# Per-head sums in an RWKV-7 mixer: whole-array matmuls and transposes replaced by matmuls in strips of TensorE

## Chip, cores and metric

One core of a Trainium2 chip runs the whole kernel. The metric is device time in microseconds (us) of one execution, as the median of the runs shown.

## What is computed

The reference is one decoder layer on 256 tokens with 2048 features: an input projection feeds two mixers side by side (a causal pooling mixer and an RWKV-7 time mixing with 16 heads of 64 features), an output projection, a squared-ReLU MLP and a gated embedding follow. The change is in the RWKV mixer, which needs two sums over the 64 features of each head, for every token:

```python
kk = hs(k * k_k)
kk = kk / jnp.maximum(jnp.linalg.norm(kk, axis=-1, keepdims=True), 1e-12)
...
y = y + jnp.sum(r_h * k_h * r_k, axis=-1, keepdims=True) * v_h
```

The first gives one norm per head and token, by which all 64 features of the head are divided. The second gives one number per head and token, which multiplies all 64 features of v. Both are a sum over a head and then a spread back over it.

## The kernel before

**Layout.** The 16 heads are worked in two groups (gi = 0, 1) of eight heads. A tensor of a group is a tile of 128 partitions x 4 x 256: partitions are features, two heads (64 + 64) in each of the four blocks p, and the 256 columns are tokens. A sum over a head is therefore a sum over 64 partitions, which TensorE does with a matmul against ones.

**Big products.** Weights arrive in tiles of 128x1024 f32 by DMA (load_raw, L155). `split_w` splits each into a rounded high part (ScalarE, L163) and a remainder (VectorE, L164), both of type fp32r, and three products of high and low parts make one f32-like product (L176 to L178 with 256 moving columns, L185 to L187 with 512). wh, wl and raw come from rings of three tiles. `split_sb` (L168, L169) splits an activation the same way: a copy on ScalarE, then a subtraction on VectorE.

**Order of the work.** TensorE's order is written by hand (`manual_schedule` for PE). The big products are generators in a queue; `fill(us)` takes the next steps of the queue until their nominal times add up to us, and so puts big-product matmuls between two steps of the mixer; `finish(g)` takes all steps up to the end of g. A step of `gemm_cols` is three matmuls of 256 columns (nominal 0.36), one of `gemm_toks` is three of 512 columns (nominal 0.68). The order of ScalarE and VectorE is made by a planner at build time, from the order in the text and from priorities; `tc.high_priority(n)` moves work forward (weight splits have 20000, the steps of the key norms 30000, and most other work of the mixer none). `inverse` is a long VectorE computation that runs beside the big products (`beside`, `pace`). PSUM has two pools of four banks each: `mm_bank` for the big products, and `rw_bank` for the mixer, whose four banks are handed out in turn.

**Key norms** (`rwkv_k`). ScalarE squares k\*k_k into sq (L512) and loads the table of the square root (L513). After fill(5.4), eight matmuls (L524) take the squares as the stationary operand, 128 tokens at a time, and multiply with jhead, 128x2, a column of ones for each of two heads: tokens become partitions, and the result is 128x16. On it come a maximum (L527), a square root (L528) and a reciprocal (L529). After fill(3.2) two transposes (L533) turn it to 8x256, `split_sb` splits it, and after fill(1.8) eight matmuls with hsel (8x512, L543 and L544) spread each of the eight rows over the 64 partitions of its head, into two banks. VectorE multiplies each block of k with its part (L548).

**r\*k\*r_k** (`rwkv_r` makes the products in st["rk"], L585; `rwkv_values` sums them). In `rwkv_values`, sixteen records of matmuls with cen (v minus its mean over the head) go to two banks called vt (L699), which ScalarE copies to UV (L701). Then `block_sum` multiplies the 128x1024 products with jsum, a 128x128 matrix with ones in the two blocks of a head (L463): one f32 matmul of 512 columns for each half sums and spreads at once. VectorE multiplies the two results with v (L706). Only `rwkv_out` needs that, much later.

**Calls.** `rwkv_k(0)` follows the product zk0 and has zr0 as its filling; `rwkv_k(1)` has zr1. `rwkv_values(0)` stands behind the end of zr1 and of the inverse of group 0, with zp0 as filling; `rwkv_values(1)` behind `rwkv_merge(1)`, with zp1 as filling. `rwkv_core` follows some time after each.

Of the kernel before, what the change touches and what calls it, by code (L numbers as in the profile page):

```python
# [9 lines left out]
F32 = mybir.dt.float32  # L10
F32R = mybir.dt.float32r
AF = mybir.ActivationFunctionType
ALU = mybir.AluOpType
# [3 lines left out]
T = 256  # L17
# [23 lines left out]
def trunk(  # L41
# [19 lines left out]
    nc = tc.nc  # L61
# [7 lines left out]
    mc = rctx.enter_context(tc.tile_pool(name="mc", bufs=1))  # L69
# [4 lines left out]
    def rw_bank(name):  # L74
        return psr.tile([128, 512], F32, tag="rw", name=name)
# [5 lines left out]
    def col(name, j):  # L81
        o = PARAM_COLS[name] + j
        return par_sb[:, o : o + 1]
# [8 lines left out]
    ident = const.tile([128, 128], F32, name="ident")  # L92
    make_identity(nc, ident)
    ones = const.tile([128, 128], F32, name="ones")
    nc.vector.memset(ones, 1.0)
    jsum = mc.tile([128, 128], F32, name="jsum")
    cmask = mc.tile([128, 128], F32, name="cmask")
    rmask = mc.tile([128, T], F32, name="rmask")
    sbd = [mc.tile([128, 4, 128], F32, name=f"sbd{i}") for i in range(2)]
    make_block_diagonal(nc, cmask, 64)  # L100
    nc.gpsimd.tensor_copy(jsum, cmask)
    cen = mc.tile([128, 128], F32, name="cen")
    nc.vector.scalar_tensor_tensor(cen, jsum, -1.0 / 64.0, ident, op0=ALU.mult, op1=ALU.add)
    jhead = mc.tile([128, 2], F32, name="jhead")
    nc.gpsimd.tensor_copy(jhead, cmask[:, ::64])
    for r0 in (0, 64):
        make_upper_triangular(nc, cmask[r0 : r0 + 64, 0:64], val=1.0, diag=False)
        make_upper_triangular(nc, cmask[r0 : r0 + 64, 64:128], val=1.0, diag=True)
# [58 lines left out]
    def split_sb(h_ap, l_ap, src_ap):  # L167
        nc.scalar.activation(h_ap, src_ap, AF.Copy)  # L168
        nc.vector.tensor_tensor(l_ap, src_ap, h_ap.bitcast(F32), op=ALU.subtract)  # L169
# [67 lines left out]
    def advance():  # L237
        try:
            us = next(queue[0])
            pace(us)  # L240
            return us
        except StopIteration:
            queue.pop(0)
            return 0.0

    def fill(us):

        while us > 0 and queue:
            us -= advance()
# [42 lines left out]
    rp = rctx.enter_context(tc.tile_pool(name="rp", bufs=1))  # L292

    def e4(tag):
        return rp.tile([128, 4, T], F32, tag=tag, name=f"{tag}_t")

    hsel_f = rp.tile([8, 512], F32, tag="BKt", name="hsel_f")
    nc.gpsimd.memset(hsel_f, 1.0)
    nc.gpsimd.affine_select(hsel_f, hsel_f, [[1, 512]], ALU.is_ge, 0.0, base=0, channel_multiplier=-64)
    nc.gpsimd.affine_select(hsel_f, hsel_f, [[-1, 512]], ALU.is_ge, 0.0, base=63, channel_multiplier=64)  # L300
    hsel = mc.tile([8, 512], F32R, name="hsel")
    nc.gpsimd.tensor_copy(hsel, hsel_f)

    def flat(t_):
        return t_.rearrange("p a t -> p (a t)")
# [148 lines left out]
    def pair_tile(tag, name, **kw):  # L454
        t_ = rp.tile([128, 2, 512], F32R, tag=tag, name=name, **kw)
        return t_[:, 0, :], t_[:, 1, :]

    def block_sum(src, name, consume):

        s = flat(src)  # L460
        for hf in range(2):
            b = rw_bank("bsum")
            nc.tensor.matmul(b, jsum, s[:, hf * 512 : (hf + 1) * 512], start=True, stop=True)  # L463
            consume(hf, b)
# [42 lines left out]
    def rwkv_k(gi, st, zk):  # L507
        P, EI, aa = st["P"], st["EI"], st["aa"]
        sq, kkn, k2 = e4("tF"), e4("tB"), e4("tE")
        with tc.high_priority(30000):  # L510
            for p in range(4):
                nc.scalar.activation(sq[:, p, :], zk[:, p, :], AF.Square, scale=col("k_k", 4 * gi + p))  # L512
        nc.scalar.activation(warm, sq[:, 3, 0:1], AF.Sqrt)  # L513

        fill(5.4)
        nb = rw_bank("kkn")
        for hf in range(2):
            h = flat(sq)[:, hf * 512 : (hf + 1) * 512]
            for j in range(2):
                for tt in range(2):  # L520
                    o = tt * 8 + (2 * hf + j) * 2
                    ts_ = slice(j * T + tt * 128, j * T + (tt + 1) * 128)
                    first = hf == 0 and j == 0 and tt == 0
                    nc.tensor.matmul(nb[:, o : o + 2], h[:, ts_], jhead, start=first, stop=True, skip_group_check=True)  # L524
        rn = rp.tile([128, 16], F32, tag="rn", name=f"rn{gi}")
        with tc.high_priority(30000):
            nc.vector.tensor_scalar_max(rn, nb[:, 0:16], 1e-24)  # L527
            nc.scalar.activation(rn, rn, AF.Sqrt)  # L528
            nc.vector.reciprocal(rn, rn)  # L529
        fill(3.2)  # L530
        nb = rw_bank("rnT")
        for tt in range(2):
            nc.tensor.transpose(nb[0:8, tt * 128 : (tt + 1) * 128], rn[:, tt * 8 : tt * 8 + 8], ident)  # L533
        rnh, rnl = (t_[0:8, 0:T] for t_ in pair_tile("tE", f"rnp{gi}"))
        with tc.high_priority(30000):
            split_sb(rnh, rnl, nb[0:8, 0:T])
        fill(1.8)
        for half in range(2):
            b = rw_bank("rnb")
            for j in range(2):  # L540
                p = half * 2 + j
                o = b[:, j * T : (j + 1) * T]
                nc.tensor.matmul(o, hsel[:, p * 128 : (p + 1) * 128], rnh, start=j == 0, stop=False, skip_group_check=True)  # L543
                nc.tensor.matmul(o, hsel[:, p * 128 : (p + 1) * 128], rnl, start=False, stop=True, skip_group_check=True)  # L544
            for j in range(2):
                p = half * 2 + j
                with tc.high_priority(30000):
                    nc.vector.scalar_tensor_tensor(  # L548
                        kkn[:, p, :], zk[:, p, :], col("k_k", 4 * gi + p), b[:, j * T : (j + 1) * T], op0=ALU.mult, op1=ALU.mult
                )  # L550
# [140 lines left out]

    def rwkv_values(gi, st, zv):

        uvs = [rp.tile([128, 2, 8, 64], F32, tag=f"q{i}", name=f"UV{gi}_{i}") for i in range(2)]
        UV = [uvs[c // 2][:, c % 2] for c in range(4)]
        for tt in range(2):
            b = rw_bank("vt")
            for p in range(4):
                nc.tensor.matmul(b[:, p * 128 : (p + 1) * 128], zv[:, p, tt * 128 : (tt + 1) * 128], cen, start=True, stop=True)  # L699
            for i in range(2):  # L700
                nc.scalar.activation(flat3(UV[2 * tt + i])[64:128], b[i * 64 : (i + 1) * 64, :], AF.Copy)  # L701
        bon = st["rk"]
        bf, vf = flat(bon), flat(zv)
        block_sum(
            st["rk"], f"rk{gi}",
            lambda hf, b: nc.vector.tensor_tensor(  # L706
                bf[:, hf * 512 : (hf + 1) * 512], b, vf[:, hf * 512 : (hf + 1) * 512], op=ALU.mult
            ),
        )
        st["UV"] = UV  # L710

    def rwkv_core(gi, st):
# [88 lines left out]
    def flat3(t_):  # L801
        return t_.rearrange("s h i -> s (h i)")
# [588 lines left out]
```

## Time and profile before

| | |
|---|---|
| median of three runs (lowest, highest) | 1204.59 us (1203.06, 1206.01) |
| profiled execution: its time | 1204.86 us |
| its span, first to last instruction | 1203.1 us |
| mean granted clock of TensorE | 0.997 |
| instructions | 18401 |

The profile comes from one execution. Engines are PE (TensorE matmuls), PEld (its weight loads), DVE (VectorE), ACT (ScalarE), POOL (GpSimd) and SP (the DMA queue's engine). A row of instructions gives start and duration in us, engine, line, operation, output <- inputs, shapes, a count, and in brackets the idle time before it and what ended it. A row of a group gives the shapes and count, then busy us and mean ns of one, then idle time before and its causes. A row of the chain gives start, duration and what ran. Matmuls are pipelined, so the time that one takes in a row of them is the distance between two starts and not its duration. A stretch of the chain has this distance in it.

### The profile page before, as it was taken

Reading aid. Unit: us, or ns where it says so; the run is one execution under the profiler, and the core shown is the slowest. Engines: PE = TensorE matmul, PEld = TensorE weight load, DVE = VectorE, ACT = ScalarE, POOL = GpSimd, SP = SyncE. Lnnn points to the kernel's source line nnn. Section 1 sums busy time; section 2 is a strip of 40 time slices with the busy share of each in tenths; the row PEclk is TensorE's granted clock in tenths of the full one; section 3 lists DMA queues with packets and bytes.
Section 4 is the critical chain, followed back from the end, with each engine's and each line's share of the span. In section 5 each row is a group of like instructions: output and inputs, shape, how many; then the busy total and the mean of one; then the engine's idle time right before and its main releaser. Section 6 shows DMA issues by size and latency. Waiting matters only on the chain.

```text
span 1203.1 us, 18401 instructions
## 1 busy us (share of the span) xinstructions
PE 1183.2 (98%) x7070; PEld 1015.0 (84%) x7070; DVE 872.9 (73%) x1186; ACT 674.7 (56%) x1203; POOL 15.5 (1%) x65
## 2 busy tenths in 40 slices
PE   7999999999999999999999999999999999999997
PEld 5999988987888888888888888888888887887886
DVE  6887987964566666666878887666667788788753
ACT  5957556565545545555545554555555555468743
POOL 3100000000000000000000000000000000000000
PEclk9999999999999999999999999999999999999999
DMA  7363543354365565565656666665565666666841
GB/s 275 124 195 113 175 141 107 107 187 142 120 211 175 175 192 184 185 191 180 192 200 205 206 194 217 185 191 181 187 192 168 194 205 204 229 203 200 271 139 70
DMA packets 60616, 216.88 MB, mean 180 GB/s; under 512 B 6768, under 2 KB 7536, under 8 KB 60144
## 3 DMA queue, kind: packets, MB, share of 16 engines
q1 hardware_dynamic: 60240, 215.20, 55.5%
q8 instruction: 55, 0.90, 0.3%
q10 hardware_dynamic: 288, 0.51, 0.1%
q14 instruction: 33, 0.27, 0.1%
HBM read 213.59 MB, written 2.10 MB: 179 GB/s over the span
## 4 chain that ended last, share of the span: by engine, by line
PE 89%; DVE 6%; DMA 2%; ACT 2%; issue 1%; ACTq 0%; DVEq 0%
PE u_w L1016 20%; PE d_p L1085 15%; PE u_w L1020 10%; PE d_w L1085 4%; PE d_d L1085 4%; DMA raw_d<-in_w_ffn_down_dram 2%; PE gt_b L187 2%; PE gt_b L186 2%; PE gt_b L185 2%; PE wag_b L346 1%; PE zp_b L185 1%; PE zv_b L176 1%; PE zp_b L187 1%; PE zp_b L186 1%; PE o_b L186 1%; PE o_b L185 1%
## 5 line engine op out<-in xcount | busy, mean ns | idle before, releaser
L1016 PE MATMUL u_w<-h,wh_u 128*128 128x512 f32 x1024 | 362.1, 399 | 0.0
L1020 PE MATMUL u_w<-h,wl_u 128*128 128x256 f32 x1024 | 287.7, 281 | 0.0
L164 DVE TENSOR_TENSOR wl_u<-raw_u,wh_u 128x1024 fp32r<-128x1024 f32 x128 | 156.7, 1224 | 122.2 <-ACT wh_u L163 122.2
L163 ACT ACTIVATE wh_u<-raw_u 128x512 fp32r<-128x512 f32 x256 | 147.6, 624 | 173.4 <-issue 137.0
L1016 PEld LDWEIGHTS u_w<-h,wh_u 128*128 128x128 f32 x1024 | 192.4, 188 | 47.9
L1020 PEld LDWEIGHTS u_w<-h,wl_u 128*128 128x128 f32 x1024 | 193.4, 189 | 0.0
L1085 PE MATMUL d_p<-wh_d,yd 128*128 128x512 f32 x480 | 154.5, 389 | 0.8 <-ACT wh_d L163 0.8
L163 ACT ACTIVATE wh_d<-raw_d 128x512 fp32r<-128x512 f32 x160 | 89.1, 620 | 36.8 <-issue 18.5
L1085 PEld LDWEIGHTS d_p<-wh_d,yd 128*128 128x128 f32 x480 | 90.1, 188 | 20.0 <-ACT wh_d L163 1.2
L164 DVE TENSOR_TENSOR wl_d<-raw_d,wh_d 128x1024 fp32r<-128x1024 f32 x80 | 95.4, 1220 | 14.3 <-ACT wh_d L163 13.9
L1085 PE MATMUL d_p<-wl_d,yd 128*128 128x512 f32 x240 | 93.6, 390 | 0.0
L1085 PE MATMUL d_d<-wh_d,yd 128*128 128x512 f32 x160 | 55.8, 389 | 0.0
L1085 PEld LDWEIGHTS d_p<-wl_d,yd 128*128 128x128 f32 x240 | 45.1, 188 | 9.7 <-DVE wl_d L164 0.6
L1138 ACT ACTIVATE th_d<-t_d 128x1024 fp32r<-128x1024 f32 x24 | 25.4, 1058 | 47.6 <-DVE t_d L1135 30.2
L1085 PE MATMUL d_w<-th_d,ys 128*128 128x512 f32 x144 | 48.2, 389 | 0.0
L1142 ACT ACTIVATE th_d<-t_d 128x1024 fp32r<-128x1024 f32 x24 | 25.4, 1059 | 35.4 <-DVE t_d L1140 31.2
L1143 DVE TENSOR_TENSOR tl_d<-t_d,th_d 128x1024 fp32r<-128x1024 f32 x24 | 29.4, 1225 | 19.9 <-ACT th_d L1142 19.6
L1132 ACT ACTIVATE w7h_d<-raw_d 128x1024 fp32r<-128x1024 f32 x24 | 25.4, 1059 | 23.4 <-DMA raw_d<-in_w_ffn_down_dram 13.8
L187 PE MATMUL gt_b<-wh_gt,h 128*128 128x512 f32 x96 | 37.8, 393 | 0.0
L176 PE MATMUL zv_b<-hTh,wh_zv 128*128 128x256 f32 x128 | 37.7, 294 | 0.0
L176 PE MATMUL zr_b<-hTh,wh_zr 128*128 128x256 f32 x128 | 37.5, 293 | 0.0
L185 PE MATMUL gt_b<-wh_gt,h 128*128 128x512 f32 x96 | 37.5, 390 | 0.0
(582 smaller groups left out, 2622.8 us busy)
## 6 DMA issues: line engine op xcount, KB each, us to landing
raw_u<-in_w_ffn_up_dram SPq DMA_DIRECT2D x128, 512.0 KB, 3.5
raw_d<-in_w_ffn_down_dram SPq DMA_DIRECT2D x128, 512.0 KB, 3.9
raw_gt<-in_w_ple_gate_dram SPq DMA_DIRECT2D x24, 512.0 KB, 4.2
raw_zk<-in_w_in_dram SPq DMA_DIRECT2D x16, 512.0 KB, 3.4
raw_zr<-in_w_in_dram SPq DMA_DIRECT2D x16, 512.0 KB, 3.5
raw_zv<-in_w_in_dram SPq DMA_DIRECT2D x16, 512.0 KB, 3.4
raw_zp<-in_w_in_dram SPq DMA_DIRECT2D x16, 512.0 KB, 3.4
raw_o<-in_w_out_dram SPq DMA_DIRECT2D x16, 512.0 KB, 4.1
```

The costliest lines, as they stand in the source:

```text
L163: nc.scalar.activation(wh[:, a * 512 : (a + 1) * 512], raw[:, a * 512 : (a + 1) * 512], AF.Copy)
L164: nc.vector.tensor_tensor(wl, raw, wh.bitcast(F32), op=ALU.subtract)
L176: nc.tensor.matmul(o, w_h, ah, start=first and ct % 2 == 0, stop=False, skip_group_check=True)
L185: nc.tensor.matmul(o, a_h, wh[:, 0:n], start=first, stop=False)
L186: nc.tensor.matmul(o, a_h, wl[:, 0:n], start=False, stop=False)
L187: nc.tensor.matmul(o, a_l, wh[:, 0:n], start=False, stop=last)
L1016: nc.tensor.matmul(bank[:, ct, :].rearrange("p (s t) -> p s t", s=2), wh[:, c], hl, start=k == 0, stop=False, skip_group_check=True,)
L1020: nc.tensor.matmul(bank[:, ct, 0:T], wl[:, c], hl[:, 0, :], start=False, stop=k == 15, skip_group_check=True)
L1085: nc.tensor.matmul(o, l, r, start=first, stop=last, skip_group_check=True)
L1132: nc.scalar.activation(ha, ra, AF.Copy)
L1138: nc.scalar.activation(th[0], t[0], AF.Copy)
L1143: nc.vector.tensor_tensor(tl[1], t[1], th[1].bitcast(F32), op=ALU.subtract)
```

## The change

- `block_sum`, jsum and the two transposes go. `jhead` becomes 128x32, with zeros beyond its first two columns; `hsel` becomes 128x128, in each 32 rows of which the first two hold ones for the two heads of a block.
- `head_sums` makes four f32 matmuls of 256 columns, one for each block p, with jhead stationary; block p's result goes to partitions 32p to 32p+31 of one bank (a column strip). The result is 128x256, of which two rows in each 32 are used.
- `head_spread` takes the two halves h and l of such a tile. For each half and each p it multiplies rows 32p to 32p+31 (a row strip) with the same rows of hsel, into four banks, first all four of h, then all four of l.
- `rwkv_k`: maximum, root, reciprocal and split now work on 128x256 directly; the fills 3.2 and 1.8 become one of 4.6 between the split and the spread.
- `rwkv_values`: the r\*k\*r_k sums stand first, then `split_sb` without priority, fill(2.0), the spread, and four products with v of 128x256 in place of two of 128x512; vt follows.

```diff
-    jsum = mc.tile([128, 128], F32, name="jsum")
...
-    nc.gpsimd.tensor_copy(jsum, cmask)
...
-    nc.vector.scalar_tensor_tensor(cen, jsum, -1.0 / 64.0, ident, op0=ALU.mult, op1=ALU.add)
-    jhead = mc.tile([128, 2], F32, name="jhead")
-    nc.gpsimd.tensor_copy(jhead, cmask[:, ::64])
+    nc.vector.scalar_tensor_tensor(cen, cmask, -1.0 / 64.0, ident, op0=ALU.mult, op1=ALU.add)
+    jhead = mc.tile([128, 32], F32, name="jhead")
+    nc.gpsimd.memset(jhead, 0.0)
+    nc.gpsimd.tensor_copy(jhead[:, 0:2], cmask[:, ::64])
...
-    def block_sum(src, name, consume):
...
+    def head_sums(src, name):
+
+        b = rw_bank(name)
+        for p in range(4):
+            nc.tensor.matmul(b[p * 32 : (p + 1) * 32, 0:T], jhead, src[:, p, :], start=True, stop=True)
+        return b[:, 0:T]
+
+    def head_spread(h, l, name):
+
+        banks = [rw_bank(f"{name}{p}") for p in range(4)]
+        for part in (h, l):
+            for p in range(4):
+                r = slice(p * 32, (p + 1) * 32)
+                nc.tensor.matmul(banks[p][:, 0:T], hsel[r], part[r], start=part is h, stop=part is l)
+        return [b[:, 0:T] for b in banks]
...
+        nb = head_sums(sq, "kkn")
+        rn = rp.tile([128, T], F32, tag="rn", name=f"rn{gi}")
+        rnh, rnl = (t_[:, 0:T] for t_ in pair_tile("tE", f"rnp{gi}"))
         with tc.high_priority(30000):
-            nc.vector.tensor_scalar_max(rn, nb[:, 0:16], 1e-24)
+            nc.vector.tensor_scalar_max(rn, nb, 1e-24)
             nc.scalar.activation(rn, rn, AF.Sqrt)
             nc.vector.reciprocal(rn, rn)
...
+            split_sb(rnh, rnl, rn)
+        fill(4.6)
+        rnb = head_spread(rnh, rnl, "rnb")
+        for p in range(4):
+            with tc.high_priority(30000):
+                nc.vector.scalar_tensor_tensor(
+                    kkn[:, p, :], zk[:, p, :], col("k_k", 4 * gi + p), rnb[p], op0=ALU.mult, op1=ALU.mult
...
     def rwkv_values(gi, st, zv):
 
+        bon = st["rk"]
+        nb = head_sums(bon, "bsum")
+        bp = rp.tile([128, 2, T], F32R, tag="sq", name=f"bs{gi}")
+        bh, bl = bp[:, 0], bp[:, 1]
+        split_sb(bh, bl, nb)
+        fill(2.0)
+        for p, b in enumerate(head_spread(bh, bl, "bon")):
+            nc.vector.tensor_tensor(bon[:, p, :], b, zv[:, p, :], op=ALU.mult)
...
-        bon = st["rk"]
-        bf, vf = flat(bon), flat(zv)
-        block_sum(
```

More of the change, by code (lines that the diff above doesn't have):

```diff
@@ L295, in e4 @@
         return rp.tile([128, 4, T], F32, tag=tag, name=f"{tag}_t")
-    hsel_f = rp.tile([8, 512], F32, tag="BKt", name="hsel_f")
+    hsel_f = rp.tile([128, 128], F32, tag="BKt", name="hsel_f")
     nc.gpsimd.memset(hsel_f, 1.0)
-    nc.gpsimd.affine_select(hsel_f, hsel_f, [[1, 512]], ALU.is_ge, 0.0, base=0, channel_multiplier=-64)
-    nc.gpsimd.affine_select(hsel_f, hsel_f, [[-1, 512]], ALU.is_ge, 0.0, base=63, channel_multiplier=64)
-    hsel = mc.tile([8, 512], F32R, name="hsel")
+    for p in range(4):
+        hs_ = hsel_f[p * 32 : (p + 1) * 32]
+        nc.gpsimd.affine_select(hs_, hs_, [[1, 128]], ALU.is_ge, 0.0, base=0, channel_multiplier=-64)
+        nc.gpsimd.affine_select(hs_, hs_, [[-1, 128]], ALU.is_ge, 0.0, base=63, channel_multiplier=64)
+    hsel = mc.tile([128, 128], F32R, name="hsel")
     nc.gpsimd.tensor_copy(hsel, hsel_f)
@@ L456, in pair_tile @@
         return t_[:, 0, :], t_[:, 1, :]
-    def block_sum(src, name, consume):
[L460 to L464, printed above, removed]
+    def head_sums(src, name):
[10 more added lines that the diff above has]
+        return [b[:, 0:T] for b in banks]
     def prod3(o, lh, ll, rh, rl, first=True, last=True):
@@ L515, in rwkv_k @@
         fill(5.4)
[L516 to L524, printed above, removed]
@@ L525, in rwkv_k @@
-        rn = rp.tile([128, 16], F32, tag="rn", name=f"rn{gi}")
+        nb = head_sums(sq, "kkn")
+        rn = rp.tile([128, T], F32, tag="rn", name=f"rn{gi}")
+        rnh, rnl = (t_[:, 0:T] for t_ in pair_tile("tE", f"rnp{gi}"))
         with tc.high_priority(30000):
-            nc.vector.tensor_scalar_max(rn, nb[:, 0:16], 1e-24)
+            nc.vector.tensor_scalar_max(rn, nb, 1e-24)
             nc.scalar.activation(rn, rn, AF.Sqrt)
             nc.vector.reciprocal(rn, rn)
-        fill(3.2)
@@ L531, in rwkv_k @@
[L531 to L549, printed above, removed]
+            split_sb(rnh, rnl, rn)
@@ L550, in rwkv_k @@
+        fill(4.6)
+        rnb = head_spread(rnh, rnl, "rnb")
+        for p in range(4):
+            with tc.high_priority(30000):
+                nc.vector.scalar_tensor_tensor(
+                    kkn[:, p, :], zk[:, p, :], col("k_k", 4 * gi + p), rnb[p], op0=ALU.mult, op1=ALU.mult
                 )
@@ L701, in rwkv_values @@
                 nc.scalar.activation(flat3(UV[2 * tt + i])[64:128], b[i * 64 : (i + 1) * 64, :], AF.Copy)
-        bon = st["rk"]
-        bf, vf = flat(bon), flat(zv)
-        block_sum(
[L705 to L709, printed above, removed]
         st["UV"] = UV
```

## The prediction

> **What bounds the kernel.** I began with the page: busy times, then the shares of the chain that ended last.
>
> ```profile
> PE 1183.2 (98%) x7070; PEld 1015.0 (84%) x7070; DVE 872.9 (73%) x1186; ACT 674.7 (56%) x1203; POOL 15.5 (1%) x65
> PE 89%; DVE 6%; DMA 2%; ACT 2%; issue 1%; ACTq 0%; DVEq 0%
> ```
>
> TensorE (PE) is busy for 98% of the span and is 89% of the chain. So PE time that goes is time won, and any new wait of PE is time lost, wherever it stands. Next, the busy times by stage where the change works (columns: stretch, length, busy PE, PEld, DVE, ACT, POOL, granted clock, DMA share, GB/s).
>
> ```profile
> 140.00:150.00 10.00, 9.20 (x75) 8.62 (x74) 9.69 (x23) 6.80 (x14) 0.00 (x0) 1.00 0.47 171
> 150.00:156.00 6.00, 6.00 (x38) 5.87 (x38) 6.00 (x9) 3.72 (x8) 0.24 (x1) 0.72 0.37 117
> 164.00:176.00 12.00, 12.00 (x70) 9.43 (x70) 10.28 (x17) 7.97 (x15) 0.00 (x0) 1.00 0.40 132
> 262.00:283.00 21.00, 21.00 (x272) 16.99 (x271) 6.07 (x10) 11.85 (x22) 0.00 (x0) 1.00 0.26 88
> ```
>
> The key norms of head group 1 fall at 140 to 150 us, where DVE has 0.31 us of 10 free; the r\*k\*r_k sums of group 0 at 164 to 176, where DVE and ACT are also well filled; those of group 1 at 262 to 283, where DVE has 15 us free. The second row has a granted clock of 0.72. The timeline of PE shows what came before it.
>
> ```profile
> 148.56 0.38 PE L543 MATMUL rnb<-rnp,hsel 8*128 8x256 f32 x1
> 149.61 0.38 PE L544 MATMUL rnb<-rnp,hsel 8*128 8x256 f32 x1 [0.67 <-DVE rnp L169]
> ...
> 151.93 0.28 PE L177 MATMUL zr_b<-hTl,wh_zr 128*128 128x256 f32 x1
> 152.05 0.33 PE L178 MATMUL zr_b<-hTh,wl_zr 128*128 128x256 f32 x1
> 152.17 0.41 PE L176 MATMUL zr_b<-hTh,wh_zr 128*128 128x256 f32 x1
> ...
> 155.37 0.37 PE L176 MATMUL zr_b<-hTh,wh_zr 128*128 128x256 f32 x1
> 155.58 0.28 PE L177 MATMUL zr_b<-hTl,wh_zr 128*128 128x256 f32 x1
> ```
>
> Matmuls of 256 columns follow each other every 0.12 us (151.93, 152.05). At 148.56 PE waits 1.05 us for DVE's half of the split norms, 0.93 more than its pace. From 152.17 to 155.37 the pace is 0.21: 3.2 us for work of about 1.8, a loss of 1.4. So a wait of about 1 us cost 0.93 + 1.4 us. The rule beside it, from the Trainium skill, "TensorE: Matmul & The Clock Gate", Part 1 (The HAM clock gate): the clock halves after an idle window of about 3.4 us. Here 1.05 us of waiting was followed by the low clock, so the trace is harsher than the page.
>
> **The change on PE.** What goes, per head group:
>
> ```profile
> 59.18 1.68 PE kkn L524 x16
> 64.20 0.22 PE rnT L533 x2
> 66.49 0.38 PE L543 MATMUL rnb<-rnp,hsel 8*128 8x256 f32 x1
> 67.62 0.39 PE L176 MATMUL zr_b<-hTh,wh_zr 128*128 128x256 f32 x1
> 164.25 1.78 PE vt L699 x16
> 166.03 1.72 PE bsum L463 x4
> ```
>
> Norm sums 1.68, transposes about 0.2 (two of the four records stand in the row; the phase's neighbours leave no more), spread 67.62 - 66.49 = 1.13, r\*k\*r_k sums 1.72: 4.73 us. Each f32 matmul is two records (8 matmuls, x16).
>
> What comes: four f32 matmuls of 256 columns in four column strips (head_sums), and eight split ones of 256 columns in four row strips (head_spread), each twice per group. The trace has strips already.
>
> ```profile
> 239.62 1.73 PE gt L835 x8
> 241.35 1.06 PE gt L839 x8
> 202.65 0.62 PE sm L767 x16
> 203.27 0.93 PE rym L780 x16
> ```
>
> L835 and L839 are four f32 matmuls of 256 columns each; L835 uses the whole array, L839 alternates between two 32-row strips: 1.06 against 1.73. L767 alternates between two column halves, L780 stays in one: 0.62 against 0.93 for the same 16 records. So strips do overlap. 1.06 is five of L835's eight 0.216 us passes: the two records of one matmul go one after the other, and the second overlaps the next strip's first. The same order is in head_sums, so I take 1.06, and 0.2 for the seams around a strip phase (an estimate: the spread's 1.13 is 0.17 more than eight steps of 0.12): 1.26. For the spread I take 0.61 (1.06 / 1.73) of 1.13, or 0.7, seams included as in the 1.13. New: 2 x 1.26 + 2 x 0.7 = 3.9 us. Saved 0.8 per group, **-1.6 us** in all.
>
> Bounds: with all four strips at once, sums 1.73 / 4 + 0.2 = 0.63 and spread 1.13 / 4 + 0.2 = 0.48, so 2.2 per group and -5.0 in all. With no overlap, 1.93 and 1.33, so 6.5 per group and +3.6. I take the middle, nearest to L839. For the upper bound speaks the Trainium skill, "TensorEngine Tiling (Array Packing)", Key Properties: changing the tiling mode drains TensorE. The change has eight strip phases.
>
> **The change on DVE and ACT.** The norms now stand as 128x256 instead of 128x16.
>
> ```profile
> L529 DVE RECIPROCAL rn<-rn 128x16 f32<-128x16 f32 x2 | 0.5, 252 | 0.7 <-ACT rn L528 0.7
> L811 DVE RECIPROCAL gv<-gv 128x8 f32<-128x8 f32 x4 | 0.7, 185 | 1.7 <-ACT gv L810 1.7
> L548 DVE SCALAR_TENSOR_TENSOR tB_t<-zk_t,par_sb,rnb 128x256 f32<-128x256 f32 x8 | 3.3, 464 | 0.7 <-PE rnb L544 0.7
> L169 DVE TENSOR_TENSOR hTl<-tA_t,hTh 128x256 fp32r<-128x256 f32 x4 | 1.6, 424 | 0.4 <-ACT hTh L168 0.2
> L168 ACT ACTIVATE hTh<-tA_t 128x256 fp32r<-128x256 f32 x4 | 1.6, 417 | 0.6 <-DVE tA_t L404 0.5
> ```
>
> Eight more columns cost the reciprocal 67 ns, 8.4 ns each; 240 more give 252 + 2016 = 2.27 us. If the cost levels off it is that of another 128x256 operation, 0.42. I take 2.0, near the slope. The chain from sums to spread is then maximum 0.46, square root 0.42, reciprocal 2.0, copy 0.42, subtraction 0.42: 3.7 us on free engines, and fill(4.6) is 13 steps of three matmuls, 4.7 us of cover. On free engines nothing waits. But the engines have queues.
>
> ```profile
> 141.74 2.36 DVE L164 TENSOR_TENSOR wl_zr<-raw_zr,wh_zr 128x1024 fp32r<-128x1024 f32 x2
> 142.77 1.28 ACT L513 ACT_TABLE_LOAD   x1
> 144.02 0.17 DVE L527 TENSOR_SCALAR rn<-kkn 128x16 f32<-128x16 f32 x1
> 144.93 0.25 DVE L529 RECIPROCAL rn<-rn 128x16 f32<-128x16 f32 x1
> 147.31 2.00 DVE L661 STREAM_TRANSPOSE T1G<-X 32x512 f32<-32x512 f32 x2
> 149.17 0.39 DVE L169 TENSOR_TENSOR rnp<-rnT,rnp 8x256 fp32r<-8x256 f32 x1
> ```
>
> Key norms, group 1: PE ends the sums near 141.9, and the maximum stays behind two weight splits and the root behind the table load, so the reciprocal begins near 145 and ends near 147. Copy and subtraction follow, the latter behind one split of 1.2 us: ready at 148.4 to 149. PE arrives at 141.9 + 5 = 146.9. The four high-half spreads cover 0.3. New wait about 1.5 against 0.93 now: **+0.6**, from -2.3 (no wait, no low clock) to +2. Behind the subtraction stand the weight splits of the next products; behind the wait of ACT's k2 scaling (L552) stands the next rounding of weights. The ring of three weight tiles hides that; without it PE would be late by as much as they are, which the +2 holds. Key norms, group 0: sums end near 60.4, PE arrives at 65.1, and the 3.7 on free engines end at 64.1; one weight split ahead on DVE (1.2, half the row) and one rounding ahead on ACT (0.6, half of L701's row below) make it 65.9: **+0.8** (0 to 2.3, more if the clock falls).
>
> **r\*k\*r_k.** Before, nothing on PE waited for its sums. Now PE computes sums, waits for ACT's rounding and DVE's subtraction, spreads, and only then does vt; fill(2.0) gives three steps of 0.7 us. Neither half of the split has raised priority. What stands in ACT's and DVE's queues there:
>
> ```profile
> 165.93 1.04 ACT L669 ACTIVATE SC<-tmp 32x1024 f32<-32x1024 f32 x1
> 167.35 1.06 ACT L669 ACTIVATE SC<-tmp 32x1024 f32<-32x1024 f32 x1
> 168.42 1.19 ACT L701 ACTIVATE UV<-vt 64x512 f32<-64x512 f32 x2
> 168.32 1.21 DVE L577 TENSOR_TENSOR AR<-zr_t,tA_t 128x1024 f32<-128x1024 f32 x1
> 169.46 1.26 DVE L585 SCALAR_TENSOR_TENSOR tF_t<-zr_t,par_sb,tE_t 128x256 f32<-128x256 f32 x3
> 170.65 1.27 DVE L706 TENSOR_TENSOR ybuf<-bsum,zv_t 128x512 f32<-128x512 f32 x2
> ```
>
> The first half of vt (L701's input) is done near 165.1, yet ACT came to it at 168.42; L706's is done at 167.75, and DVE came at 170.65. The split takes the same places: rounding at 168.4, subtraction between 169.3 and 171. PE starts the sums at 164.25, ends them at 165.5 and the fill at 167.6. Wait 1.7 to 3.7; I take 3.0, and with it a low clock of 1.4 to 1.5: **+4.5** (0 to +5.3). All of PE's products stand behind it. Group 1 (262 to 283) has idle DVE and ACT: 0. In both groups vt takes the bank of the first spread, so it waits for one product of 0.43 (L548's size, less what the last spreads cover): 0.3 each, **+0.6**. The bank sums' own DVE work grows from two 128x512 to four 128x256 products, beside PE. The POOL edits at the start, and the weights of `cen`, are needed tens of us later: 0; uncovered they would cost a few tenths.
>
> Sum: -1.6 + 0.6 + 0.8 + 4.5 + 0.6 = +4.9. The profiled execution took 1204.86 us, 1.76 of them outside its span of 1203.1: 1209.8. It lies 0.27 above the median 1204.59, so the forecast for a median is **1209.5**.
>
> **Rivals.**
> Queues let the split through. If ACT and DVE take the r\*k\*r_k split about as it comes, the 4.5 falls to about 1: 1206. For it: DVE has 1.7 us free in 164 to 176. Against: L701 and L706.
>
> Strips pay and all covers hold, ending faster: -1.6 or up to -5.0, the present wait and low clock gone (-2.3), +0.6: 1201 to 1198. For it: 3.7 against 4.7 on free engines. Against: the subtraction now comes 7 us after the sums (142.2 to 149.17). The Trainium skill, "TensorE: Matmul & The Clock Gate", Measured speedup vs the span model, has four row strips 3.07 times as fast; by it the sums would take 1.73 / 3.07 = 0.56 us, an estimate, and this rival would be nearer its lower end. No run here shows four strips.
>
> The strips don't overlap, so the change doesn't do what it says: PE +3.6 in place of -1.6, so 1214.7. Against: L839, L767. The Trainium skill's same page, Part 3, What overlaps and what doesn't, lets weights load beside a matmul only in another row group, which would hold for the column strips; L767's 0.62 against 0.93 speaks otherwise.
>
> Low clock three times: the norms of group 0 also wait over 1 us: 1209.5 + 1.4 = 1211.
>
> **How the numbers follow.** Forecast 0.45 (own range 1207 to 1212.5), queues let it through 0.26, pays 0.12, no overlap 0.09, low clock three times 0.08. Range 1202 to 1214: it leaves out most of "no overlap" and the lower end of "pays". A measurement tells about 0.3%, 3.6 us, from no change: slower means above 1208.2, faster below 1201. Slower: 0.38 of the forecast and 0.09 + 0.08, 0.55. Faster: most of "pays", 0.09. Same: 0.36.
>
> **What would show it.** L524's successor near 1.06 us on the chain; a reciprocal of 128x256 near 2 us; PE waiting for DVE's subtraction of the r\*k\*r_k sums near 168 us, and a granted clock below 1 behind it; none near 270. It is wrong if the planner puts that split ahead of L669 and L585, or the reciprocal takes 0.4.

## The result, and the profile after

The changed kernel takes 1212.74 us (median of 5 runs, 1211.58 to 1214.21), the kernel before 1204.59 (1200.28 to 1206.2 in 5): a ratio of 1.0073 [1.0051, 1.0096], so 8.15 us lost. The profiled execution took 1212.74 us, 1211.0 of them span. The busy times of the page:

```profile
PE 1182.3 (98%) x7074; PEld 1012.2 (84%) x7074; DVE 876.4 (72%) x1192; ACT 676.3 (56%) x1205; POOL 18.0 (1%) x71
```

PE's busy time is 0.9 us less than before, in a span that is 7.9 longer. The loss is not work: it is waiting, and a lower clock behind the wait. The view of PE's waits in the changed kernel (what waited for what: us in total, times, longest):

```profile
...
PE bon L472 <- DVE bs L168: 5.3, 1, 5.3
...
PE vt L696 <- DVE tF_t L690: 1.1, 1, 1.1
PE rnb L472 <- ACT rnp L167: 1.0, 1, 1.0
...
PE rnb L472 <- DVE rnp L168: 0.7, 1, 0.7
```

The line of bon is the prediction's wait: the spread of the r\*k\*r_k sums (bon) stands until DVE has subtracted the high half (bs). The same stretches as before the change:

```profile
140.00:150.00 10.00, 7.57 (x57) 6.42 (x55) 9.76 (x19) 6.83 (x13) 0.00 (x0) 0.95 0.56 174
150.00:156.00 6.00, 6.00 (x43) 6.00 (x43) 5.68 (x8) 3.41 (x7) 1.10 (x2) 0.81 0.44 144
164.00:176.00 12.00, 6.36 (x32) 5.22 (x31) 9.04 (x17) 3.74 (x7) 0.00 (x0) 0.73 0.27 87
262.00:283.00 21.00, 19.92 (x224) 16.72 (x223) 9.37 (x14) 9.94 (x19) 0.00 (x0) 1.00 0.43 142
```

In the third stretch PE was busy for 12 us of 12 before, now 6.36, and the granted clock fell from 1.00 to 0.73. To put the loss in its place, compare where the same work starts on PE (us from the span's start):

| start of | before | after | shift | gained or lost since the row above |
|---|---|---|---|---|
| norm sums, group 0 | 59.02 | 59.03 | 0 | |
| norm sums, group 1 | 140.71 | 139.49 | -1.2 | -1.2: norms of group 0 |
| r\*k\*r_k and vt, group 0 | 164.09 | 163.11 | -1.0 | +0.2: norms of group 1 |
| scores, group 1 | 175.21 | 183.90 | +8.7 | +9.7: r\*k\*r_k of group 0 |
| merge (qm), group 1 | 266.76 | 275.93 | +9.2 | +0.5 |
| h2t of the next stage | 357.64 | 365.44 | +7.8 | -1.4: r\*k\*r_k of group 1 and GEMM steps left |
| end | 1203.1 | 1211.0 | +7.9 | +0.1 |

Of the +9.7, 2.1 us are three GEMM steps that the new fill(2.0) brings forward; they come back in the row of -1.4, which is +0.7 of its own less these 2.1. So one place lost about 7.6 us. The timeline of PE there, and of DVE and ACT in the same microseconds:

```profile
163.11 0.64 PE L463 MATMUL bsum<-ybuf,jhead 128*32 128x256 f32 x8
...
165.96 0.39 PE L472 MATMUL bon<-bs,hsel 32*128 32x256 f32 x3
171.68 0.79 PE L472 MATMUL bon<-bs,hsel 32*128 32x256 f32 x5 [5.33 <-DVE bs L168]
172.78 3.68 PE L696 MATMUL vt<-cen,zv_t 128*128 128x128 f32 x16 [0.31 <-DVE ybuf L690]
```

```profile
165.09 1.19 DVE L163 TENSOR_TENSOR wl_zp<-raw_zp,wh_zp 128x1024 fp32r<-128x1024 f32 x1
166.21 0.46 DVE L311 SCALAR_TENSOR_TENSOR zr_t<-zr_b,par_sb,zr_t 128x255 f32<-128x255 f32 x1
166.60 0.46 DVE L574 SCALAR_TENSOR_TENSOR tF_t<-zr_t,par_sb,tE_t 128x256 f32<-128x256 f32 x1
166.99 1.21 DVE L566 TENSOR_TENSOR AR<-zr_t,tA_t 128x1024 f32<-128x1024 f32 x1
168.12 1.26 DVE L574 SCALAR_TENSOR_TENSOR tF_t<-zr_t,par_sb,tE_t 128x256 f32<-128x256 f32 x3
169.31 2.04 DVE L654 STREAM_TRANSPOSE tmp<-X 64x512 f32<-64x512 f32 x2
171.26 0.37 DVE L168 TENSOR_TENSOR bs<-bsum,bs 128x256 fp32r<-128x256 f32 x1
```

```profile
165.23 0.39 ACT L167 ACTIVATE bs<-bsum 128x256 fp32r<-128x256 f32 x1
171.39 2.12 ACT L658 ACTIVATE SC<-tmp 32x1024 f32<-32x1024 f32 x2 [5.76 <-DVE tmp L654]
```

Read the three together. ACT has the high half ready near 165.6, and PE uses it at 165.96 for three of the four blocks (x3). The fourth, by the order in which banks are handed out, goes to the bank of the sums, which DVE's subtraction still has to read, and then come the four of the low half, which the subtraction makes (x5). That subtraction takes DVE 0.37 us, but stands last in DVE's order, behind 5.6 us of work that PE has no use for yet. PE moves again at 171.68, and vt then takes 3.44 us (172.78 to 176.22, where the next GEMM record starts) for 1.78 before. The low clock behind the wait (stretches of the changed kernel, the clock is the third number from the right):

```profile
170.00:175.00 5.00, 3.01 (x15) 2.72 (x16) 3.04 (x7) 2.11 (x2) 0.00 (x0) 0.50 0.00 0
175.00:180.00 5.00, 5.00 (x25) 4.35 (x24) 1.04 (x1) 2.36 (x5) 0.00 (x0) 0.88 0.02 3
```

PE is busy for 3.01 us of the first stretch and for all of the second, so the low clock costs about 3.01 x 0.5 + 5 x 0.12 = 2.1 us.

The strips themselves do what they say, and more than I counted. The sums of group 0's norms and what follows them on PE, the spread in group 1, and the reciprocal in the view of the tile rn (ns: shortest/median/longest):

```profile
59.03 0.64 PE L463 MATMUL kkn<-tF_t,jhead 128*32 128x256 f32 x8
59.60 0.38 PE L175 MATMUL zr_b<-hTh,wh_zr 128*128 128x256 f32 x1
...
280.90 0.51 PE L472 MATMUL bon<-bs,hsel 32*128 32x256 f32 x8
```

```profile
L531 DVE RECIPROCAL rn<-rn x2: 1746/1750/1753, 62.1 to 145.2; 128x256 f32<-128x256 f32 x2
```

A phase of sums takes 0.57 us (59.03 to 59.60), a phase of spread 0.51 (the length of its row; PE waits behind it). That holds where PE finds its inputs ready. At the norms it does not always: the spread of group 0 lasts from 64.74 to 65.59, 0.85 us, and the sums of group 1 last 1.00, because the squares of their last block come late from ACT. PE then waits for a weight split that it now reaches sooner:

```profile
64.74 0.93 PE L472 MATMUL rnb<-rnp,hsel 32*128 32x256 f32 x8
65.59 0.39 PE L175 MATMUL zr_b<-hTh,wh_zr 128*128 128x256 f32 x1
...
139.49 1.06 PE L463 MATMUL kkn<-tF_t,jhead 128*32 128x256 f32 x8
140.49 0.39 PE L175 MATMUL zr_b<-hTh,wh_zr 128*128 128x256 f32 x1
...
141.72 0.39 PE L177 MATMUL zr_b<-hTh,wl_zr 128*128 128x256 f32 x1 [0.73 <-DVE wl_zr L163]
```

### The profile page after: what moved, and what is told of

Its sections match the earlier page's. It is cut to its first block, busy times and chain, and to the rows that moved or that the text cites. A ratio compares the mean times of both kernels' runs of the same rounds, so it can differ in the third digit from the quotient of the medians.

```text
span 1211.0 us, 18418 instructions
## 1 busy us (share of the span) xinstructions
PE 1182.3 (98%) x7074; PEld 1012.2 (84%) x7074; DVE 876.4 (72%) x1192; ACT 676.3 (56%) x1205; POOL 18.0 (1%) x71
## 4 chain that ended last, share of the span: by engine, by line
PE 70%; DVE 3%; DMA 2%; ACT 1%; issue 0%; DVEq 0%; ACTq 0%
PE u_w L1005 20%; PE d_p L1074 14%; PE u_w L1009 10%; PE d_w L1074 4%; PE d_d L1074 4%; DMA raw_d<-in_w_ffn_down_dram 2%; PE gt_b L185 2%; PE gt_b L184 2%; PE gt_b L186 2%; PE o_b L185 1%; PE o_b L184 1%; PE o_b L186 1%; DVE wl_d L163 0%; PE o0a_b L184 0%; DVE w7l_d L1122 0%
## 5 line engine op out<-in xcount | busy, mean ns | idle before, releaser
L177 PE MATMUL zr_b<-hTh,wl_zr 128*128 128x256 f32 x128 | 37.1, 290 | 0.7 <-DVE wl_zr L163 0.7
```

Of the source, the lines that this page charges most:

```text
L177: nc.tensor.matmul(o, w_l, ah, start=False, stop=last, skip_group_check=True)
```

## The experiments

The theory I took to the chip: the loss is the **order of DVE's queue** at the r\*k\*r_k sums of group 0, where the split has no priority, plus the low clock behind the wait; the strips gain. A further guess hung on it: that the two long reciprocals of the norms (1.75 us each) push the inverse's last transposes (L654) in front of that subtraction and make the wait longer. Rivals: DVE is simply full there, and order only decides who waits; the strip phases or the longer chain of the norms cost the time.

### e1_prio_split_prod: priority for the split and the products

```diff
-        split_sb(bh, bl, nb)
+        with tc.high_priority(30000):
+            split_sb(bh, bl, nb)
...
-            nc.vector.tensor_tensor(bon[:, p, :], b, zv[:, p, :], op=ALU.mult)
+            with tc.high_priority(30000):
+                nc.vector.tensor_tensor(bon[:, p, :], b, zv[:, p, :], op=ALU.mult)
```

> The split of the r*k*r_k sums and the four products behind it get raised priority, in both groups; nothing else changes. Theory (order of DVE's queue): PE's wait of 5.3 us for the subtraction in group 0 falls below 1 us, the low clock behind it goes too; 1212.7 - 5.3 - 2.5 to 3 = about 1204 to 1205. Rival (DVE is full, the order only decides who waits): the inverse's last transposes land later by what the split and the products take (about 0.4 + 4 x 0.4 us), PE waits for them elsewhere before the scores, and the time stays within 2 us of 1212.7. Rival (the strip phases themselves cost): the wait goes, but the time stays above 1208.

Measured: 1204.43 us, ratio to the kernel before 1.0 [0.999, 1.0011]. The whole loss of 8.3 us against 1212.74 is gone. PE's timeline in this kernel:

```profile
161.02 0.64 PE L463 MATMUL bsum<-ybuf,jhead 128*32 128x256 f32 x8
...
163.86 0.51 PE L472 MATMUL bon<-bs,hsel 32*128 32x256 f32 x8
...
165.65 2.05 PE L698 MATMUL vt<-cen,zv_t 128*128 128x128 f32 x16 [1.28 <-DVE ybuf L692]
```

and DVE's, where the subtraction and the products now stand ahead of the transposes:

```profile
163.34 0.40 DVE L168 TENSOR_TENSOR bs<-bsum,bs 128x256 fp32r<-128x256 f32 x1
...
165.19 1.40 DVE L692 TENSOR_TENSOR ybuf<-bon,zv_t 128x256 f32<-128x256 f32 x4
...
170.82 2.29 DVE L654 STREAM_TRANSPOSE tmp<-X 64x512 f32<-64x512 f32 x2
```

No wait in front of the spread, none of the low clock (1.00 in every stretch from 140 to 185). PE did not wait for the later transposes elsewhere. The theory holds, and the rival "the wait only moves" falls for the large wait. What is left is 1.28 us at vt here and 1.1 in group 1.

### e11_prio_split: the same for the split alone

```diff
-        split_sb(bh, bl, nb)
+        with tc.high_priority(30000):
+            split_sb(bh, bl, nb)
```

> The changed kernel with raised priority for the split alone, not for the products behind it. Theory (DVE's order decides for each link of the chain): PE's wait of 5.3 us in front of the spread goes, but vt now waits for the bank of the first spread, whose product stands behind the same last transposes of the inverse on DVE until about 171 us, so PE waits 4 us or more at vt with the low clock behind it, and the time stays at 1210 to 1212.7. Rival (the split alone was what stood late): 1204 to 1205, level with e1_prio_split_prod.

Measured: 1212.66 us, ratio 1.0072 [1.0058, 1.0086]. PE in this kernel:

```profile
166.94 0.51 PE L472 MATMUL bon<-bs,hsel 32*128 32x256 f32 x8
...
173.00 3.78 PE L697 MATMUL vt<-cen,zv_t 128*128 128x128 f32 x16 [5.55 <-DVE ybuf L691]
```

The spread is on time, and vt waits 5.55 us for its bank in place of 5.33 for the split: the product that frees the bank stands behind the same transposes. Each link of the chain must have its place in DVE's order; mending one moves the wait to the next, at the same price.

### e2_norms_only, e3_values_only: one half of the change at a time

Norms alone; `rwkv_values`, block_sum and jsum are those of before the change:

```diff
-        bon = st["rk"]
-        nb = head_sums(bon, "bsum")
...
+        block_sum(
+            st["rk"], f"rk{gi}",
```

> Only the key norms take the strips; the r*k*r_k sums are as before the change. Theory: the norms gained 1.2 us in group 0 and lost 0.2 in group 1, so 1203 to 1204.5, and the first scores of group 1 start within 2 us of the kernel before. Rival (the longer chain of the norms delays the inverse, and that is the loss): 1207 or more, with a new PE wait behind the inverse's last transposes.

Measured: 1201.42 us, ratio 0.9976 [0.9965, 0.9987]: **faster than both kernels**, by 2.9 us against the one before. What the longer chain of the norms costs in waits (1.0 and 0.7 us in group 1) is less than what the strips win there.

r\*k\*r_k alone; the key norms, with 128x2 and 8x512 constants of their own, are those of before the change:

```diff
-        nb = head_sums(sq, "kkn")
...
+                    nc.tensor.matmul(nb[:, o : o + 2], h[:, ts_], jhead2, start=first, stop=True, skip_group_check=True)
...
-        rnb = head_spread(rnh, rnl, "rnb")
...
+                nc.tensor.matmul(o, hsel8[:, p * 128 : (p + 1) * 128], rnh, start=j == 0, stop=False, skip_group_check=True)
```

> Only the r*k*r_k sums take the strips; the key norms are as before the change. Theory: the wait for the subtraction in group 0 stays, at about 3 us since the inverse's last transposes stand earlier in DVE's queue, with a low clock behind it: 1208 to 1210. If the norms have no part in that wait: 5.3 us again and about 1213. If the wait needs the norms (they alone push the transposes in front of it): below 1 us and about 1203.

Measured: 1211.24 us, ratio 1.0057 [1.0044, 1.007]. PE in this kernel:

```profile
168.34 0.39 PE L481 MATMUL bon<-bs,hsel 32*128 32x256 f32 x3 [2.59 <-ACT bs L169]
170.65 0.79 PE L481 MATMUL bon<-bs,hsel 32*128 32x256 f32 x5 [1.92 <-DVE bs L170]
```

The wait is 4.5 us, not 3. It needs nothing of the norms. Here the transposes were early (DVE ended the last at 165.3), and other work stood in front of the subtraction just the same: it starts at 170.19. The two halves do not add: -2.9 and +7.0 make +4.1, and the change costs 8.15. The norms bring PE to the r\*k\*r_k sums earlier, but there the end of the wait is set by DVE, which lets PE go at 170.65 here and at 171.68 in the changed kernel. What PE gains ahead of such a wait is lost in it.

### e4_no_division

```diff
-            nc.vector.reciprocal(rn, rn)
+            nc.vector.tensor_scalar_mul(rn, rn, 4e-7)
```

> The changed kernel with the reciprocal of the norms (2 x 1.75 us on DVE) replaced by a multiplication by a constant (about 0.25 to 0.4 us each): the division is left out, so the keys are scaled by a constant times their norm. Theory: DVE wins about 1.4 us per group, the inverse's last transposes move ahead of where they stood, PE's wait in group 0 falls from 5.3 to about 3, the waits at the norms of group 1 (1.0 + 0.7) go: about 1207 to 1209. If the reciprocal has no part in it: only the waits at the norms go, 1211. If the reciprocal is all of it: 1203.

Measured: 1210.29 us, ratio 1.0048 [1.0035, 1.006]. PE in this kernel:

```profile
166.06 0.58 PE L472 MATMUL bon<-bs,hsel 32*128 32x256 f32 x3 [4.36 <-ACT bs L167]
168.44 0.79 PE L472 MATMUL bon<-bs,hsel 32*128 32x256 f32 x5 [1.79 <-DVE bs L168]
```

My further guess falls. The transposes did move forward, and the waits at the norms went, but the wait at the spread became 6.2 us: now ACT's rounding came late as well, behind the copies of the inverse's result (L658), which have their input sooner. PE arrives 4 us earlier than in the changed kernel and is let go 3.2 us earlier (168.44 for 171.68). Wherever the inverse's transposes stand in the three kernels whose split has no priority (the changed one, r\*k\*r_k alone, no division), DVE comes to the subtraction only after the r products.

### e8_no_strips

The same sums and spreads on the whole array, on top of the priorities of the first experiment (jfull has the two columns of jhead at 96, hfull is hsel with all rows of the other strips zero):

```diff
-        for p in range(4):
-            nc.tensor.matmul(b[p * 32 : (p + 1) * 32, 0:T], jhead, src[:, p, :], start=True, stop=True)
+        for p in (3, 0, 1, 2):
+            nc.tensor.matmul(b[0 : (p + 1) * 32, 0:T], jfull[:, 96 - p * 32 :], src[:, p, :], start=p == 3, stop=p == 2, skip_group_check=True)
...
-                nc.tensor.matmul(banks[p][:, 0:T], hsel[r], part[r], start=part is h, stop=part is l)
+                nc.tensor.matmul(banks[p][:, 0:T], hfull[:, p, :], part, start=part is h, stop=part is l)
```

> The kernel of e1_prio_split_prod with the same matmuls on the whole array: the sums have 128 rows of weights and up to 128 columns that are zero but for one head pair and accumulate in one bank, the spread has 128 rows of weights that are zero but for one strip; the results are the same. Theory (four strips work at the same time: a phase of sums takes 0.57 us against 1.7, a phase of spread 0.6 to 0.85 against 1.1): four phases of each cost 4 x 1.15 + 4 x 0.4 = about 6 more, so 1210, less what they shorten the waits for the split and for the bank, 1208 to 1210. Rival (the strips save nothing, the gain of the norms is the missing transposes): 1204 to 1205.

Measured: 1211.76 us, ratio 1.0066 [1.0049, 1.0082]; 7.3 us more than with strips. Sums and spread in this kernel:

```profile
59.08 2.32 PE L468 MATMUL kkn<-tF_t,jfull 128*128 128x256 f32 x8
61.06 0.47 PE L175 MATMUL zr_b<-hTh,wh_zr 128*128 128x256 f32 x1
...
171.12 1.11 PE L476 MATMUL bon<-bs,hfull 128*128 128x256 f32 x8
```

1.98 us for 0.57, and about 1.1 for 0.51: four phases of each make 4 x (1.41 + 0.6) = 8.0, which the 7.3 nearly are (the waits shift too: 2.3 + 0.6 us for 1.0 + 1.0 at the norms, 0.4 + 0.5 for 1.3 + 1.1 at vt; and the clock of 150 to 156 us is 0.72 for 1.00). So the strips are worth their price: they gain in the order of 7 us over the same matmuls without them. (The old r\*k\*r_k sums needed no spread, and so are not what this compares with.)

### e5, e6, e7: more GEMM steps in the gaps

Three kernels try to close what is left of the waits by moving queued GEMM steps into them. In the first, fill(1.4) stands between the spread and vt of the kernel with priorities; in the second, fill(4.6) of the norms becomes fill(6.3) in the kernel with the norms alone; the third has both edits on the kernel with priorities.

```diff
+        fill(1.4)
         uvs = [rp.tile([128, 2, 8, 64], F32, tag=f"q{i}", name=f"UV{gi}_{i}") for i in range(2)]
...
-        fill(4.6)
+        fill(6.3)
```

> The kernel of e1_prio_split_prod with 1.4 us of queued GEMM steps put between the spread of the r*k*r_k sums and the products with cen (vt), in both groups. Theory (what is left of the loss is vt's wait for the bank that the first spread holds until its product is done, 1.28 us in group 0 and 1.08 in group 1): both waits go and 1204.4 falls by about 2.4 to 1202. Rival (the steps that fill the gap are missing later as cover, in the group's core): a new wait of about the same size there, and 1204.

> The kernel of e2_norms_only (key norms in strips, r*k*r_k as before the change) with fill(6.3) in place of fill(4.6) between the sums and the spread of the norms, in both groups. Theory: the waits of 1.0 and 0.7 us for the split of the norms in group 1 and 0.3 in group 0 go: 1201.4 falls by about 1.5 to 2 to 1199.5. Rival (the inverse's first steps and the scores start later and are late instead, or the steps are missing later): 1201 or more.

> Both of the last two edits on the changed kernel with raised priority: fill(6.3) in the norms and 1.4 us of GEMM steps ahead of vt. Theory: the two gains add, 1204.4 - 2.4 - 1.7 = about 1200.3, level with the norms alone in strips. If the strips also gain in r*k*r_k: below 1199. If cover is short: 1202 or more.

Measured: 1204.99 us (ratio 1.0009 [0.9998, 1.002]), 1201.62 (0.998 [0.9967, 0.9994]) and 1203.42 (1.0002 [0.9989, 1.0014]). None gains on its base (1204.43, 1201.42 and 1204.43) what the waits had promised. The profile of the second shows one way in which that happens. The norms alone, two stretches:

```profile
150.00:160.00 10.00, 10.00 (x85) 10.00 (x84) 10.00 (x11) 5.00 (x10) 1.10 (x2) 1.00 0.47 156
160.00:170.00 10.00, 10.00 (x54) 8.08 (x53) 10.00 (x16) 4.20 (x9) 0.00 (x0) 1.00 0.41 135
```

DVE is busy for all of these 20 us. With the larger fill PE no longer waits at the norms; then, in the view of PE's waits and in the stretch behind it:

```profile
PE sc L602 <- DVE ybuf L705: 1.3, 1, 1.3
```

```profile
175.00:180.00 5.00, 5.00 (x28) 3.77 (x28) 1.70 (x3) 3.22 (x10) 0.00 (x0) 0.71 0.38 113
```

The scores of group 1 wait 1.3 us for a bank that DVE's product holds, with a clock of 0.71 behind it. The gap was closed and opened again 25 us later. In this execution the rival is right for these last 1 to 2 us: from 150 to 170 us **DVE is the second bound**, and work that PE does in one gap opens another. In the third kernel the wait came back at the spread itself:

```profile
164.23 0.50 PE L472 MATMUL bon<-bs,hsel 32*128 32x256 f32 x5 [1.06 <-DVE bs L168]
```

That PE's gaps can't be closed at all is not shown. The profiles of the first and the third kernel come from executions of 1209.55 and 1209.91 us, 4.6 and 6.5 above their medians, and that excess stands in a stage that no edit touches: from the first d_w to the first pp_b (the second product of the MLP, long after the mixer) they take 508.3 and 510.6 us, the kernel with priorities 503.8. Where the edits act, from the norm sums of group 0 to h2t, the third takes 296.4 us for 298.2 in its base, so there the moved steps closed part of the gaps; its median shows 1.0 us. The first takes 298.9 for 298.2: its waits at vt are down from 2.4 to 0.5 us, but its clock was 0.91 and 0.87 from 140 to 156 us.

### e9, e10: r\*k\*r_k in strips where DVE is free

The norms in strips, and r\*k\*r_k in strips in group 1 alone (products with priority), without and with fill(1.4) ahead of vt:

```diff
+        if gi == 1:
+            nb = head_sums(bon, "bsum")
...
+                with tc.high_priority(30000):
+                    nc.vector.tensor_tensor(bon[:, p, :], b, zv[:, p, :], op=ALU.mult)
...
+        if gi == 0:
+            bf, vf = flat(bon), flat(zv)
+            block_sum(
```

> The kernel of e2_norms_only, with the r*k*r_k strips (products at raised priority) in head group 1 alone, where DVE has free time; group 0 keeps the sums over the whole array behind vt. Theory (the strips pay where DVE is free; from the merge of group 1 to the first transposes of the next stage e1_prio_split_prod took 89.5 us and e2_norms_only 90.9): 1201.4 - 1.4 = 1200.0. Rival (the added wait of vt for the bank, 1.08 us, eats what the strips save, as it did in e1_prio_split_prod over both groups): 1201 to 1202.5.

> The kernel of e9_values_g1 with 1.4 us of GEMM steps between the spread and vt in group 1. Theory: vt's wait of 1.08 us falls to 0.5 or less as in e5_fill_before_vt and 1200.0 becomes about 1199.4. Rival (the steps are missing in the group's core, as they may have been in e5_fill_before_vt): no change against e9_values_g1.

Measured: 1203.99 us (0.9997 [0.998, 1.0015]) and 1200.97 (0.9974 [0.9962, 0.9987]). The first is no better than the kernel before, the second is level with the norms alone (0.9976). So strips for r\*k\*r_k bring nothing that can be told apart, even where DVE is free. That 1.4 us of moved steps make 3 us, as the two medians have it, I can't explain: the single runs of the first lie between 1197.08 and 1206.77, and the profiles of the two show the same waits up to vt. Nor do these profiles show a gain of the second: from the norm sums of group 0 to h2t they take 296.3 and 297.1 us (the norms alone 296.1), the second with a low clock that the first did not have (below). It stays open.

## Why the prediction was right, and where its sizes were off

The forecast was 1209.5, with a range of 1202 to 1214 and "slower" as likeliest; it came to 1212.74, by the mechanism that the prediction priced, just above the 1212.5 with which the forecast's own range ended. By the number alone the rival without overlap, at 1214.7, was nearer; the runs rule it out. That the total came within 3.3 us is partly luck: the strips won more than I had taken, the wait took more, and the two errors partly cancel. The steps by stage, from the terms of its sum, beside the table above (the 2.1 us of moved GEMM steps put back where they belong):

| stage | forecast | measured |
|---|---|---|
| norms, group 0: strips -1.05, wait +0.8 | -0.25 | -1.2 |
| norms, group 1: strips -1.05, wait +0.6 | -0.45 | +0.2 |
| r\*k\*r_k, group 0: strips +0.24, wait 3.0, low clock 1.5, bank 0.3 | +5.0 | +7.6 |
| r\*k\*r_k, group 1: strips +0.24, bank 0.3 | +0.5 | +0.7 |
| in between and behind | 0 | +0.6 |

**The strips.** Mis-sized, and the largest single error of working. I read L839's 1.06 us as "the two records of one matmul go one after the other, and the second overlaps the next strip's first", and took 1.26 for the sums and 0.7 for the spread. The runs show 0.57 and 0.51 where the inputs are ready: about a third of the 1.72 of the old r\*k\*r_k sums, less than half of the old spread. Per group 2 x 0.57 + 2 x 0.51 = 2.2 in place of 4.73, -5.1 in all, which is the bound that I had called -5.0, not the -1.6 that I took. The changed kernel does not get all of it, since four of its eight phases are held up by their inputs. L839 alternates between two strips; that four would overlap further I had only as a bound. The Trainium skill, "TensorE: Matmul & The Clock Gate", Measured speedup vs the span model, gave 0.56 for the sums, an estimate by its 3.07 for four row strips; the 0.57 measured for these column strips agrees, while the row strips of the spread come to 1.11 / 0.51 = 2.2 (rows of the kernel without strips and of this one). The drain that the Trainium skill, "TensorEngine Tiling (Array Packing)", Key Properties, has for a change of the tiling mode does not show beyond 0.1 to 0.2 us in a phase (0.57 for 1.72 / 4 = 0.43; for the spread 0.44 for 1.13 / 4 = 0.28, from start to start in the third kernel with more GEMM steps, where one stands right behind it):

```profile
66.86 0.51 PE L472 MATMUL rnb<-rnp,hsel 32*128 32x256 f32 x8
67.30 0.39 PE L175 MATMUL zr_b<-hTh,wh_zr 128*128 128x256 f32 x1
```

**The norms' queue.** Right in kind. The reciprocal took 1.75 us (2.0 taken); the split was ready at 148.46 (148.4 to 149 forecast) and PE waited 1.01 + 0.69 (1.5 forecast). The 0.73 us for a weight split and the late squares of group 1 I had not: there the stage lost 0.2 us although its strips were faster than I had taken. In group 0 about 0.4 us of waiting lie inside the spread's row (0.85 for 0.44; 0.8 forecast).

**The r\*k\*r_k split.** The step of the forecast that carried it, right in place and in mechanism, too small in size. I had the subtraction between 169.3 and 171, PE there at 167.6 and a wait of 3.0. The subtraction began at 171.26, just behind the late end, and PE arrived at 166.35, because the sums took 0.57 and not 1.26 and the norms had already won 1.0. So the wait was 5.33. The error about the strips and this one belong together: PE is let go when DVE is done, and whatever PE gains ahead of that makes the wait longer. I named the r products in front of the subtraction, rightly. The inverse's copies, which I put in front of the rounding, were not there: ACT rounded at 165.23 and not at 168.4, and the copies (L658) came at 171.39. Only DVE's half was late. That the last transposes of the inverse would stand in front of it too I did not foresee, and the runs without the norms or without the division say that it makes little difference: other work takes the place. The low clock behind it cost about 2.1 us, not 1.5.

**vt and the bank.** 0.31 in group 0 (0.3 forecast), 1.08 in group 1, where a weight split of 1.2 us stood ahead of the product on DVE.

**The rivals.** "Strips don't overlap" is out by the kernel without strips. "Queues let the split through" is what the kernel with priorities makes of it: 1204.43, near the 1206 that this rival had. "Strips pay and covers hold" is near the norms alone, 1201.42, near the 1201 of its upper end. That the low clock comes three times did not happen.

What stays open: against the norms alone, the kernel with priorities takes 3.0 us more. The waits at vt (1.28 and 1.08) less what its phases save against the old sums (1.72 - 0.57 - 0.51 = 0.64 in each group) make 1.1; the other 1.9 no view puts in one place. In the two profiles, which lie 3.4 us apart, 2.2 of them stand between the norm sums of group 0 and h2t (298.2 and 296.1 us), and 0.8 between d_w and pp_b (503.8 and 503.0), where no edit acts.

## What to carry to other kernels

Before a step on the bound engine is made to wait for a small operation elsewhere, look at where that operation and every later one of the chain stand in the other engine's order; without priority, 0.4 us of work cost 5.3 us of waiting, and giving it to one link alone moved the wait to the next. A wait whose end another engine sets swallows what is won ahead of it, so two halves of a change must be measured apart: here one half was worth -2.9 us and the other +7.0. Where the second engine is full, as DVE is from 150 to 170 us, moving the first engine's work into its gaps can open them again later.

## What the runs showed of the hardware that was not expected

Four column strips of f32 matmuls, 128x32 weights and 256 columns each, work at the same time: 0.57 us for all four, against 1.98 for four matmuls with the same sums whose weights (32 to 128 columns) all begin at the same column. Four row strips, eight matmuls in two passes: a row of 0.51 us against 1.11 on the whole array.

The reciprocal costs by the column far more than other operations of its size: 1750 ns for 128x256, where the maximum of the same shape takes 414 and the subtraction 409.

The low clock after a wait of about 1 us is not certain. The last two kernels above (r\*k\*r_k in group 1, without and with fill(1.4)) are the same program up to the values of group 1, and in the norms of group 1 PE waits 1.0 and 0.7 us in both. The stretch behind it in the first and in the second:

```profile
150.00:156.00 6.00, 6.00 (x52) 6.00 (x51) 6.00 (x8) 3.54 (x7) 1.10 (x2) 1.00 0.34 113
```

```profile
150.00:156.00 6.00, 6.00 (x39) 6.00 (x39) 6.00 (x9) 3.81 (x8) 1.11 (x2) 0.72 0.47 143
```

52 matmul records against 39, at a granted clock of 1.00 and of 0.72. It is the same with the kernel before, whose single wait of 0.67 there was followed by 0.72, and r\*k\*r_k alone in strips, whose 0.66 was followed by 1.00. So the wait that the prediction made 1.4 us of low clock of costs that in one execution and nothing in another. After waits of 4 us and more, in one piece or two (the changed kernel, the split alone with priority, r\*k\*r_k alone, no division), a clock near half speed followed every time. The Trainium skill, "TensorE: Matmul & The Clock Gate", Part 1 (The HAM clock gate), has the clock halve after an idle window of about 3.4 us; the long waits agree with that, the low clock after 1 us does not. It is not what sets single runs of one kernel up to 10 us apart, as far as the profiles show: in the thirteen of them the stage from d_w to pp_b, which no edit touches, takes between 502.6 and 510.6 us, and in the longest of these the granted clock is 1.00 throughout. What makes that stage longer in some executions stays open.
